# Strassen's algorithm for the second MLP product of a two-layer network, on one core

## Chip, core and metric

One core of a Trainium2 chip runs the whole program: 512 tokens of width 1024 through one block of attention, state-space mixing and an MLP, one RG-LRU layer and one latent-attention layer. The metric is the time of one execution on the device in microseconds (us), the median of several runs.

## What is computed

The change touches the MLP of the first block and the three norms around it:

```python
h2 = rms_norm(x, norm2_w[l]) * (1.0 + scale2) + shift2
ff = jnp.square(jax.nn.relu(h2 @ w_mlp1[l])) @ w_mlp2[l]
x = x + gate2 * ff
```

`h2` is 512 x 1024, `w_mlp1` 1024 x 4096, `w_mlp2` 4096 x 1024, and all is float32. After it the RG-LRU layer takes `rms_norm(x)` again, and the latent-attention layer once more.

## The kernel before

A float32 product is made of three passes of a faster format: each operand is split into a high part (a cast on ScalarE, `wh`, `rh`) and a low part (the operand minus the high part, `wl`, `rl`), and `mm3` (L173 to L176) adds hi x hi, hi x lo and lo x hi in PSUM. Each weight tile, 128x1024 (512 KB), is loaded by SP into `wr` (L159), cast on ScalarE (L162), and its low part is subtracted on VectorE or GpSimd (L165). `lo_pool` says how many of twelve go to GpSimd; in the MLP that is none. Four buffers each of `wr`, `wh` and `wl` let loads and splits run some blocks ahead of TensorE.

The MLP (`mlp`, L973) goes in 4 chunks of 1024 hidden units. The first product of a chunk (`gemm_cm`) has 8 blocks of 24 matmuls (8 k x 3) of 128 hidden units by 512 tokens. In chunk 0 the first four blocks are done by halves of the tokens, so that the norm of the last token blocks can still come in. Each block is followed by a relu on ScalarE (L982), a square on GpSimd (L983) and the split of the result (`split`, L167). The second product (`gemm_tm`) has two column halves x 4 token blocks x 8 k x 3 = 192 matmuls of 128 tokens by 512 columns. For each of its 8 sums, `resid` (L944) multiplies by the row of gates (L949) and adds to `x` (L950) on VectorE.

`token_norm` (L281) turns one block of 128 tokens of `x` into operands of the next product: two `xn` on GpSimd (L290), transposes on TensorE (L294), scaling and split. `half_stats` makes the sums that it needs (L322 to L328). `h2` is such an operand pair (two tiles, high and low), as are `ha` for RG-LRU and `hb` for latent attention; `norm2`, `norm3` and `norm4` make them.

No scheduler reorders: each engine runs its instructions in the order in which the program writes them, and waits for what they read and for their buffers. SP issues all loads in that order too. Pools (`phase`) decide what memory a tile reuses and so what it waits for.

Of the kernel before, what the change touches and what calls it, by code (L numbers as in the profile page):

```python
# [59 lines left out]
class Build:  # L60
# [1463 lines left out]
```

## Time and profile before

| what | value |
|---|---|
| median of 3 runs | 1649.78 us (1648.66 to 1652.85) |
| profiled execution | 1649.19 us, span 1647.4 us |
| mean granted clock of TensorE | 0.993 |
| busy: TensorE, VectorE, ScalarE, GpSimd | 96%, 68%, 48%, 27% |
| MLP, first matmul of product 1 to the end of chunk 3 | 867.5 to 1221.7 us |

A share is an average over the whole span. The MLP is some 354 us of it, and the views by stretch tell how busy each engine is there. In the rows below PE is TensorE's matmuls and PEld its weight loads, DVE is VectorE, ACT is ScalarE, POOL is GpSimd and SP issues loads; `out<-in` names the tiles, and an arrow behind a time names what ended the idle time before the instruction.

### The profile page before, as it was taken

Reading aid. Unit: us, or ns where it says so; the run is one execution under the profiler, and the core shown is the slowest. Engines: PE = TensorE matmul, PEld = TensorE weight load, DVE = VectorE, ACT = ScalarE, POOL = GpSimd, SP = SyncE. Lnnn points to the kernel's source line nnn. Section 1 sums busy time; section 2 is a strip of 40 time slices with the busy share of each in tenths; the row PEclk is TensorE's granted clock in tenths of the full one; section 3 lists DMA queues with packets and bytes.
Section 4 is the critical chain, followed back from the end, with each engine's and each line's share of the span. In section 5 each row is a group of like instructions: output and inputs, shape, how many; then the busy total and the mean of one; then the engine's idle time right before and its main releaser. Section 6 shows DMA issues by size and latency. Waiting matters only on the chain.

```text
span 1647.4 us, 20884 instructions
## 1 busy us (share of the span) xinstructions
PE 1580.8 (96%) x7696; PEld 1279.2 (78%) x7696; DVE 1128.2 (68%) x1948; ACT 789.3 (48%) x1517; POOL 446.0 (27%) x322
## 2 busy tenths in 40 slices
PE   5989999999999999999999999999999999999998
PEld 3767667677688778778888888888888778988886
DVE  7899679689868988874445343443467884747883
ACT  4356546354465667663334232232336662454652
POOL 3314335244252443431133011111141011321012
PEclk8999999999999999999999999999999999999999
DMA  7612124224222222315313333323323222322211
GB/s 254 196 52 65 52 77 128 75 72 139 91 82 80 80 62 80 96 52 183 111 52 117 101 97 95 102 90 102 105 77 99 87 90 67 100 69 69 65 63 52
DMA packets 50649, 153.54 MB, mean 93 GB/s; under 512 B 8178, under 2 KB 12914, under 8 KB 50547
## 3 DMA queue, kind: packets, MB, share of 16 engines
q1 hardware_dynamic: 50546, 152.22, 28.9%
q8 instruction: 60, 0.98, 0.3%
q14 instruction: 43, 0.34, 0.1%
HBM read 150.10 MB, written 2.10 MB: 92 GB/s over the span
## 4 chain that ended last, share of the span: by engine, by line
PE 67%; DVE 18%; ACT 4%; issue 3%; POOL 3%; DMA 1%; DVEq 0%; POOLq 0%; ACTq 0%
PE pm L175 18%; PE pm L174 18%; PE pm L176 18%; DVE acc L507 3%; DVE wl L165 1%; DVE nmax L752 1%; PE px L608 1%; PE px L848 1%; DVE w L635 1%; PE px L598 1%; DMA wada<-in_w_ada 1%; POOL rs L254 1%; PE px L857 1%; POOL wl L165 1%; PE px L856 1%
## 5 line engine op out<-in xcount | busy, mean ns | idle before, releaser
L162 ACT CAST wh<-wr 128x1024 fp32r<-128x1024 f32 (+5 forms) x245 | 239.7, 980 | 389.3 <-PE pm L175 168.9
L165 DVE TENSOR_TENSOR wl<-wr,wh 128x1024 fp32r<-128x1024 f32 (+2 forms) x170 | 203.3, 1196 | 184.8 <-ACT wh L162 183.9
L165 POOL TENSOR_TENSOR wl<-wr,wh 128x1024 fp32r<-128x1024 f32 (+3 forms) x75 | 174.7, 2330 | 532.9 <-ACT wh L162 486.6
L174 PE MATMUL pm<-hh,wh 128*128 128x512 f32 x432 | 173.8, 406 | 8.2 <-ACT hh L169 6.6
L175 PE MATMUL pm<-hl,wh 128*128 128x512 f32 x432 | 176.0, 407 | 3.9 <-POOL hl L170 3.8
L176 PE MATMUL pm<-hh,wl 128*128 128x512 f32 x432 | 172.9, 401 | 0.0
L983 POOL TENSOR_TENSOR r<-r 128x512 f32<-128x512 f32 x32 | 50.8, 1589 | 252.3 <-ACT r L982 252.3
L174 PE MATMUL pm<-h,wh 128*128 128x512 f32 (+1 forms) x288 | 105.4, 366 | 0.0
L175 PE MATMUL pm<-h,wh 128*128 128x512 f32 (+1 forms) x288 | 105.3, 365 | 0.0
L176 PE MATMUL pm<-h,wl 128*128 128x512 f32 (+1 forms) x288 | 105.2, 365 | 0.0
L174 PEld LDWEIGHTS pm<-hh,wh 128*128 128x128 f32 x432 | 81.8, 190 | 29.9 <-ACT hh L169 8.4
L175 PEld LDWEIGHTS pm<-hl,wh 128*128 128x128 f32 x432 | 82.3, 190 | 27.1 <-POOL hl L170 7.6
L174 PE MATMUL pm<-wh,rh 128*128 128x512 f32 x256 | 99.8, 390 | 0.0
L760 POOL TENSOR_SCALAR pr<-pr,psum 128x512 f32<-128x512 f32 x64 | 64.8, 1024 | 128.8 <-DVE psum L756 71.6
L176 PE MATMUL pm<-wh,rl 128*128 128x512 f32 x256 | 99.6, 389 | 0.0
L175 PE MATMUL pm<-wl,rh 128*128 128x512 f32 x256 | 99.6, 389 | 0.0
L176 PEld LDWEIGHTS pm<-hh,wl 128*128 128x128 f32 x432 | 82.4, 191 | 19.9 <-issue 3.1
L507 DVE SCALAR_TENSOR_TENSOR acc<-pm,conv_w_s,acc 128x510 f32<-128x510 f32 (+2 forms) x118 | 87.4, 741 | 8.3 <-ACT acc L498 7.3
L279 DVE SCALAR_TENSOR_TENSOR wada<-wada,cs 128x1024 f32<-128x1024 f32 x48 | 68.9, 1446 | 16.4 <-DMA wada<-in_w_ada 15.8
L643 POOL TENSOR_TENSOR e<-e,w 128x512 f32<-128x512 f32 x32 | 52.0, 1626 | 101.1 <-ACT e L642 87.0
L755 ACT ACTIVATE pr<-px,nmax 128x512 f32<-128x512 f32 (+2 forms) x96 | 60.5, 638 | 29.8 <-DVE nmax L752 23.9
L174 PE MATMUL pm<-ha,wh 128*128 128x512 f32 (+1 forms) x192 | 68.2, 355 | 0.0
(401 smaller groups left out, 4120.3 us busy)
## 6 DMA issues: line engine op xcount, KB each, us to landing
wr<-in_w_mlp SPq DMA_DIRECT2D x64, 512.0 KB, 3.5
wada<-in_w_ada SPq DMA_DIRECT2D x48, 512.0 KB, 4.0
wr<-in_w_xbc SPq DMA_DIRECT2D x24, 512.0 KB, 3.5
wr<-in_w_in_a SPq DMA_DIRECT2D x20, 512.0 KB, 3.5
wr<-in_w_z SPq DMA_DIRECT2D x16, 512.0 KB, 3.6
wr<-in_w_ssd_out SPq DMA_DIRECT2D x16, 512.0 KB, 3.6
wr<-in_w_gate SPq DMA_DIRECT2D x16, 512.0 KB, 3.7
wr<-in_w_qkv SPq DMA_DIRECT2D x16, 384.0 KB, 3.0
```

The lines of the kernel that those rows point to most:

```text
L162: nc.scalar.copy(out=hi[:, :n], in_=raw[:, :n])
L165: eng.tensor_tensor(out=lo[:, :n], in0=raw[:, :n], in1=r32(hi[:, :n]), op=ALU.subtract)
L174: m(out, lhsT=lh, rhs=rh, start=start, stop=False)
L175: m(out, lhsT=lh, rhs=rl, start=False, stop=False)
L176: m(out, lhsT=ll, rhs=rh, start=False, stop=stop)
L254: g.tensor_tensor(out=r, in0=r, in1=self.mhalf.to_broadcast(list(ss.shape)) if len(ss.shape) == 2 else self.mhalf.unsqueeze(2).to_broadcas ...
L279: nc.vector.scalar_tensor_tensor(out=w, in0=w, scalar=1.0, in1=self.cs, op0=ALU.mult, op1=ALU.mult, accum_out=self.modc[:, j:j + 1])
L507: nc.vector.scalar_tensor_tensor(out=acc[:, lo:hi], in0=ps[:, lo + o:hi + o], scalar=w[:, j:j + 1], in1=acc[:, lo:hi], op0=ALU.mult, op1=A ...
L643: self.e("ew").tensor_tensor(out=e, in0=e, in1=w, op=ALU.mult)
L755: nc.scalar.activation(out=e[:, :n], in_=p, func=AF.Exp, bias=nmax, accum_out=s)
L760: self.e("norm").tensor_scalar(out=e[:, :n], in0=e[:, :n], scalar1=s, scalar2=1.0, op0=ALU.mult, op1=ALU.mult)
L983: self.e("sq").tensor_tensor(out=r, in0=r, in1=r, op=ALU.mult)
```

## The change

The second product of each chunk becomes seven half-size products (Strassen's algorithm in Winograd's form) instead of eight. The squared hidden values `R` (1024 hidden units by 512 tokens) are cut into four quarters a11 to a22 by hidden half and token half, the weights `W0` and `W1` (the two column halves) into b11 to b22. A product is 2 token blocks x 4 k x 3 = 24 matmuls. Its two factors are made in place by additions of quarters (`combine`), and then split (`rparts`: 128x1024; `wparts`: two halves of 128x1024 each). Three of the products are added into PSUM tiles that already hold another (A and X), the rest into tiles of their own; each finished tile is added to `x` in one or two places.

The gate can no longer be multiplied into the sums, since one sum enters two column halves. It is multiplied into the raw weights on GpSimd (L1012 of the changed kernel), 8 tiles a chunk. The weights of the second product are loaded straight into `W0` and `W1`, one copy of each, so the loads of the next chunk go into quarters that the present one still reads. The low parts of R are made on VectorE for products 1 to 3 and on GpSimd for 4 to 7, all low parts of the weights on VectorE. Of the combinations, GpSimd has `a11-=a21` and the last of b11, VectorE the others.

The tiles `h2`, `ha` and `hb` share one pool of two (`hbig`). The rows of gates lie in another pool, some pools are entered at another point, pads between pools differ, and the small loads of the next layers come earlier. In the last chunk the sums are closed by token block, with the statistics and the next norm after each; the norms of token blocks 2 and 3 run inside the first product of RG-LRU. In the changed kernel the lines stand 3 lower up to the MLP (L165 becomes L168, L170 becomes L173).

```diff
-PAD = [0, 16, 56, 0, 32, 0, 32, 0, 0, 24, 0, 0, 40, 56, 32, 16, 0]
+PAD = [48, 16, 56, 0, 32, 0, 32, 32, 0, 0, 0, 0, 56, 0, 16, 0, 0]
...
+    def hbig(self, name):
+        return self.hpool.tile([128, 8, 512], F32R, tag="big", name=self.nm(name))
...
-        self.h2 = self.big("h2", F32R), self.big("h2", F32R)
+        self.h2 = self.hbig("h2"), self.hbig("h2")
...
-    def mlp(self, done):
+    def mlp(self):
...
         hh, hl = self.h2
+        R, W0, W1 = self.big("R"), self.big("W0"), self.big("W1")
+        a11, a21, a12, a22 = R[:, 0:4, 0:256], R[:, 0:4, 256:512], R[:, 4:8, 0:256], R[:, 4:8, 256:512]
+        b11, b21, b12, b22 = W0[:, 0:4], W0[:, 4:8], W1[:, 0:4], W1[:, 4:8]
+        V, P = nc.vector, nc.gpsimd
+        def rparts(x, eng):
+            hi, lo = [self.pool("x").tile([128, 4, 256], F32R, tag="x", name=self.nm(n)) for n in ("sh", "sl")]
+            self.split(hi, lo, x, eng=eng)
+            return hi, lo
+        def wparts(x, eng):
+            res = []
+            for j in (0, 2):
+                hi, lo = [self.pool(n).tile([128, 2, 512], F32R, tag=n, name=self.nm(n)) for n in ("wh", "wl")]
+                self.split(hi, lo, x[:, j:j + 2], eng=eng)
+                res += [(hi[:, k], lo[:, k]) for k in range(2)]
+            return res
+        def combine(out, x, y, op, eng, n=2):
+            for j in range(0, 4, n):
+                s = slice(j, j + n)
+                eng.tensor_tensor(out=out[:, s], in0=x[:, s], in1=y[:, s], op=op)
         for ch in range(4):
-            rt = []
+            for b, w in enumerate((W0, W1)):
+                for i in range(4):
+                    v = w[:, 2 * i:2 * i + 2]
+                    nc.sync.dma_start(out=v, in_=a["w_mlp2"][ch, b, i])
+                    gate = self.gb[40][:, b * 512:b * 512 + 512].unsqueeze(1).to_broadcast([128, 2, 512])
+                    P.tensor_tensor(out=v, in0=v, in1=gate, op=ALU.mult)
 
             def evac(m, ps):
-                with self.fills():
-                    r = self.t("r")
-                    hi, lo = self.t("rh", F32R), self.t("rl", F32R)
-                nc.scalar.activation(out=r, in_=ps, func=AF.Relu)
-                self.e("sq").tensor_tensor(out=r, in0=r, in1=r, op=ALU.mult)
-                self.split(hi, lo, r)
-                rt.append((hi, lo))
+                nc.scalar.activation(out=R[:, m], in_=ps, func=AF.Relu)
+                self.e("sq").tensor_tensor(out=R[:, m], in0=R[:, m], in1=R[:, m], op=ALU.mult)
 
             self.gemm_cm([[a["w_mlp1"][ch * 8 + m]] for m in range(8)], lambda k: (hh[:, k], hl[:, k]), evac,
-                         halves=4 if ch == 0 else 0, mid=lambda: self.norm2(3))
-            if ch == 3:
-                done()
...
-            self.gemm_tm([[a["w_mlp2"][ch, b, i] for i in range(4)] for b in range(2)], lambda k: rt[k],
-                         lambda b, t, ps: self.resid(self.gb[40], b, t, ps, self.r3 if ch == 3 else None), 512,
-                         touter=ch == 3, pre=self.trail(self.norm3) if ch == 3 else None)
+            Z, A, C, X = [[f(), f()] for f in (self.pm, self.pm, self.ps, self.ps)]
+            def product(r, w, ps, start, done):
+                (rh, rl) = r
+                order = [(j, i) for j in range(2) for i in range(2)] if not last or start else \
+                    [(j, i) for i in range(2) for j in range(2)]
+                for j, i in order:
+                    for k in (2 * j, 2 * j + 1):
+                        s = slice(i * 128, i * 128 + 128)
+                        self.mm3(ps[i], rh[:, k, s], rl[:, k, s], w[k][0], w[k][1], start and k == 0, k == 3,
+                                 skip_group_check=True)
+                    if j == 1:
+                        for tok, col in done:
+                            x = xv[:, tok * 2 + i, col * 512:col * 512 + 512]
+                            V.tensor_tensor(out=x, in0=x, in1=ps[i], op=ALU.add)
+                        if last:
+                            stats(ps, i)
+            def stats(ps, i):
+                t, n = (i, 0) if ps is C else (i, 1) if ps is X and X[0] in closing else \
+                    (i + 2, 2) if ps is A and A[0] in closing else (0, 3)
+                for b in [[0], [1], [0, 1], []][n]:
+                    self.half_stats(self.r3, xv[:, t, b * 512:b * 512 + 512], b, t)
+                if n == 2:
+                    self.norm3(i)
+            closing = []
+            combine(b12, b12, b11, ALU.subtract, V)
+            r, w = rparts(a11, V), wparts(b11, V)
+            product(r, w, A, True, [(0, 0)])
+            r, w = rparts(a12, V), wparts(b21, V)
+            product(r, w, C, True, [(0, 0)])
+            combine(a11, a11, a21, ALU.subtract, P, 4)
+            combine(a21, a21, a22, ALU.add, V, 4)
+            r, w = rparts(a21, V), wparts(b12, V)
+            product(r, w, X, True, [(1, 1)])
+            combine(b12, b22, b12, ALU.subtract, V)
+            combine(b21, b21, b12, ALU.subtract, V)
+            r, w = rparts(a22, P), wparts(b21, V)
+            product(r, w, Z, True, [(1, 0)])
+            combine(b11, b12, b11, ALU.subtract, P)
+            combine(a22, a22, a11, ALU.subtract, V, 4)
+            r, w = rparts(a22, P), wparts(b12, V)
+            product(r, w, A, False, [(0, 1)])
+            combine(a12, a12, a22, ALU.subtract, V, 4)
+            r, w = rparts(a12, P), wparts(b22, V)
+            closing = [X[0]]
+            product(r, w, X, False, [(0, 1)])
+            r, w = rparts(a11, P), wparts(b11, V)
+            closing = [A[0]]
+            product(r, w, A, False, [(1, 0), (1, 1)])
         self.dump("x2", xv)
...
-        self.hb = self.big("hb", F32R), self.big("hb", F32R)
+        self.hb = self.hbig("hb"), self.hbig("hb")
...
-                G = stack(b.phase(side="right"), tail)
-                b.gb = {j: b.c([128, 1024], f"gb{j}") for j in (16, 40)}
                 b.mh, b.ml = big("mh"), big("ml")
                 with b.fills():
                     b.merge()
                 O.close()
                 F.close()
+                H = stack(b.phase(nbig=2, side="right", bare=True), tail)
+                b.hpool = b.pool("big")
+                M = stack(b.phase(nt=NMLP, side="right"), tail)
+                b.gb = {j: b.c([128, 1024], f"gb{j}") for j in (16, 40)}
                 b.mod_cols(16, 32)
                 b.gate_rows(16, 0.5)
                 b.gate_rows(40, 1.0)
-                M = stack(b.phase(nt=NMLP, side="right"), tail)
-                H = stack(b.phase(nbig=2, side="right", bare=True), tail)
                 b.out_proj()
+            c = b.stack[0]["c"]
+            b.nkv, b.nb = b.load("norm_kv", [128, 8], pool=c), b.load("norm_b", [128, 8], pool=c)
+            b.lo_pool = LO["mlp"]
+            with b.phase(nbig=3, nx=6, bare=True):
+                b.mlp()
```

VectorE in the second product of a chunk, before: the low parts of the next first product's weights (L165), then the gates and sums.

```order
L165 TENSOR_TENSOR wl1746_8575<-wr1744_8573,wh1745_8574 128x1024
L165 TENSOR_TENSOR wl1753_8613<-wr1751_8611,wh1752_8612 128x1024
L165 TENSOR_TENSOR wl1760_8651<-wr1758_8649,wh1759_8650 128x1024
L949 TENSOR_TENSOR rt1739_8542<-pm1723_8436,gb40_6859 128x512
L949 TENSOR_TENSOR rt1740_8551<-pm1724_8437,gb40_6859 128x512
L950 TENSOR_TENSOR x1482_6847<-x1482_6847,rt1739_8542 128x512
L950 TENSOR_TENSOR x1482_6847<-x1482_6847,rt1740_8551 128x512
L949 TENSOR_TENSOR rt1741_8560<-pm1725_8438,gb40_6859 128x512
```

The same place now: product 3's weights (`wl1704`, `wl1706`), two in-place combinations of b12 (L1004 on W1) with sums of product 2 between them (L1039), b21 from b12 (on W0), a22 from a11 (on R), sums of product 3, and the first weight half of product 4 (`wl1710`).

```order
L173 TENSOR_TENSOR wl1704_8368<-W11642_7872,wh1703_8367 128x1024
L173 TENSOR_TENSOR wl1706_8372<-W11642_7872,wh1705_8371 128x1024
L1004 TENSOR_TENSOR W11642_7872<-W11642_7872 128x1024
L1039 TENSOR_TENSOR x1482_6849<-x1482_6849,px1685_8279 128x512
L1004 TENSOR_TENSOR W11642_7872<-W11642_7872 128x1024
L1039 TENSOR_TENSOR x1482_6849<-x1482_6849,px1686_8280 128x512
L1004 TENSOR_TENSOR W01641_7871<-W01641_7871,W11642_7872 128x1024 x2
L1004 TENSOR_TENSOR R1640_7870<-R1640_7870 128x4x256
L1039 TENSOR_TENSOR x1482_6849<-x1482_6849,px1687_8281 128x512
L1039 TENSOR_TENSOR x1482_6849<-x1482_6849,px1688_8282 128x512
L173 TENSOR_TENSOR wl1710_8410<-W01641_7871,wh1709_8409 128x1024
```

Six additions on SBUF operands now stand between the weights of product 3 and those of product 4.

GpSimd from the last norm ahead of the MLP, before: after the `xn` only squares follow, 32 in a row.

```order
L290 TENSOR_SCALAR xn1657_7974<-x1482_6847,r22_7476 128x512
L290 TENSOR_SCALAR xn1660_7988<-x1482_6847,r22_7476 128x512
L983 TENSOR_TENSOR r1663_8120<-r1663_8120 128x512
L983 TENSOR_TENSOR r1666_8127<-r1666_8127 128x512
L983 TENSOR_TENSOR r1669_8134<-r1669_8134 128x512
```

Now, from the squares of chunk 0 to those of chunk 1: `sl` are the low parts of R for products 4 to 7 (1708, 1714, 1720, 1726), L1004 is b11 from b12, L1012 the gates for the next chunk, first b21, then b12, b22 and b11.

```order
L1016 TENSOR_TENSOR R1640_7870<-R1640_7870 128x512 x4
L173 TENSOR_TENSOR sl1708_8406<-R1640_7870,sh1707_8405 128x1024
L1004 TENSOR_TENSOR W01641_7871<-W11642_7872,W01641_7871 128x1024 x2
L173 TENSOR_TENSOR sl1714_8447<-R1640_7870,sh1713_8446 128x1024
L1012 TENSOR_TENSOR W01641_7871<-W01641_7871,gb40_7443 128x1024 x2
L173 TENSOR_TENSOR sl1720_8486<-R1640_7870,sh1719_8485 128x1024
L1012 TENSOR_TENSOR W11642_7872<-W11642_7872,gb40_7443 128x1024
L173 TENSOR_TENSOR sl1726_8524<-R1640_7870,sh1725_8523 128x1024
L1012 TENSOR_TENSOR W11642_7872<-W11642_7872,gb40_7443 128x1024 x3
L1012 TENSOR_TENSOR W01641_7871<-W01641_7871,gb40_7443 128x1024 x2
L1016 TENSOR_TENSOR R1640_7870<-R1640_7870 128x512 x4
```

Two gates now stand ahead of product 6's low part, one ahead of product 7's, and five between that and the next chunk's squares.

VectorE at the start of the MLP, before: weights of the first product and the last parts of `h2` (the token blocks 2 and 3).

```order
L170 TENSOR_TENSOR h21573_7480<-nh1636_7840,h21572_7479 128x4x128
L165 TENSOR_TENSOR wl1653_7892<-wr1651_7890,wh1652_7891 128x1024
L170 TENSOR_TENSOR h21573_7480<-nh1639_7854,h21572_7479 128x4x128
L165 TENSOR_TENSOR wl1656_7898<-wr1654_7896,wh1655_7897 128x1024
L306 TENSOR_TENSOR nh1662_7995<-pt1661_7990,g2_7477 128x512
L309 TENSOR_TENSOR nh1662_7995<-nh1662_7995,modc_84 128x512
L170 TENSOR_TENSOR h21573_7480<-nh1659_7981,h21572_7479 128x4x128
L170 TENSOR_TENSOR h21573_7480<-nh1662_7995,h21572_7479 128x4x128
```

Now two combinations of W1 and W0 stand there; both read what GpSimd has multiplied by the gate.

```order
L173 TENSOR_TENSOR h21572_7475<-nh1638_7849,h21571_7474 128x4x128
L168 TENSOR_TENSOR wl1658_7913<-wr1656_7911,wh1657_7912 128x1024
L309 TENSOR_TENSOR nh1664_8010<-pt1663_8005,g2_7472 128x512
L1004 TENSOR_TENSOR W11642_7872<-W11642_7872,W01641_7871 128x1024
L173 TENSOR_TENSOR h21572_7475<-nh1661_7996,h21571_7474 128x4x128
L312 TENSOR_TENSOR nh1664_8010<-nh1664_8010,modc_85 128x512
L1004 TENSOR_TENSOR W11642_7872<-W11642_7872,W01641_7871 128x1024
L173 TENSOR_TENSOR h21572_7475<-nh1664_8010,h21571_7474 128x4x128
```

The low parts of `h2` for the last token block (from `nh1661` and `nh1664`) come behind them.

## Rows read from the trace of the kernel before

**Rows 1.** The page's first part: busy time, share of the span and instructions of each engine.

```profile
PE 1580.8 (96%) x7696; PEld 1279.2 (78%) x7696; DVE 1128.2 (68%) x1948; ACT 789.3 (48%) x1517; POOL 446.0 (27%) x322
```

**Rows 2.** Stretches of the MLP: stretch, length, busy us (instructions) per engine, clock, DMA share, GB/s.

```profile
913.30:956.80 43.50, 43.50 (x193) 36.04 (x192) 18.21 (x22) 9.52 (x10) 1.59 (x1) 1.00 0.30 97
956.80:1000.30 43.50, 43.50 (x193) 36.03 (x192) 16.55 (x19) 16.22 (x22) 11.13 (x7) 1.00 0.31 97
1130.90:1174.40 43.50, 43.50 (x193) 36.04 (x192) 16.52 (x19) 16.23 (x23) 11.12 (x7) 1.00 0.31 98
1174.40:1221.70 47.30, 46.35 (x218) 38.38 (x216) 27.96 (x54) 18.26 (x32) 13.17 (x18) 1.00 0.26 80
```

**Rows 3.** Waits in the MLP, 867 to 1222 us: total us, times, longest us.

```profile
POOL r L983 <- ACT r L982: 252.3, 32, 47.4
DVE wl L165 <- ACT wh L162: 132.7, 53, 4.2
ACT wh L162 <- PE pm L176: 102.1, 26, 4.4
...
PE pt L294 <- POOL xn L290: 2.3, 2, 1.3
```

**Rows 4.** Groups by line and shape, 867 to 1222 us: count, busy us, mean ns, idle before.

```profile
L174 PE MATMUL pm<-wh,rh 128*128 128x512 f32 x256 | 99.8, 390 | 0.0
...
L165 DVE TENSOR_TENSOR wl<-wr,wh 128x1024 fp32r<-128x1024 f32 x64 | 78.8, 1231 | 132.9 <-ACT wh L162 132.7 <-PE pm L175 0.3
L162 ACT CAST wh<-wr 128x1024 fp32r<-128x1024 f32 x64 | 67.3, 1054 | 158.8 <-PE pm L176 102.1 <-PE pm L175 52.6 <-issue 2.3
...
L983 POOL TENSOR_TENSOR r<-r 128x512 f32<-128x512 f32 x32 | 50.8, 1589 | 252.3 <-ACT r L982 252.3
...
L950 DVE TENSOR_TENSOR x<-x,rt 128x512 f32<-128x512 f32 x33 | 23.1, 734 | 0.0
...
L949 DVE TENSOR_TENSOR rt<-pm,gb 128x512 f32<-128x512 f32 x33 | 22.0, 685 | 9.7 <-PE pm L176 8.8
...
L982 ACT ACTIVATE r<-pm 128x512 f32<-128x512 f32 x32 | 18.9, 591 | 0.0
...
L290 POOL TENSOR_SCALAR xn<-x,r 128x512 f32<-128x512 f32 x9 | 10.5, 1173 | 0.4
```

**Rows 5.** Order of time, VectorE and GpSimd, 1440.6 to 1445.5: start us, us, instruction.

```profile
1440.69 1.21 DVE L165 TENSOR_TENSOR wl<-wr,wh 128x1024 fp32r<-128x1024 f32 x1
1441.83 1.21 DVE L161 TENSOR_TENSOR wr<-wr,norm_b_s 128x1024 f32<-128x1024 f32 x1
...
1440.88 4.41 POOL L165 TENSOR_TENSOR wl<-wr,wh 128x1024 fp32r<-128x1024 f32 x1 [4.72 <-ACT wh L162]
```

**Rows 6.** Order of time, GpSimd and VectorE, 837 to 842.

```profile
837.59 2.39 POOL L165 TENSOR_TENSOR wl<-wr,wh 128x1024 fp32r<-128x1024 f32 x1 [19.14 <-ACT wh L162]
837.77 0.69 DVE L949 TENSOR_TENSOR rt<-pm,gb 128x512 f32<-128x512 f32 x1 [4.45 <-PE pm L176]
...
838.50 2.03 DVE L950 TENSOR_TENSOR x<-x,rt 128x512 f32<-128x512 f32 x1
...
840.45 0.68 DVE L949 TENSOR_TENSOR rt<-pm,gb 128x512 f32<-128x512 f32 x1
```

**Rows 7.** The page's DMA issues: count, KB each, median us from issue to landing.

```profile
wr<-in_w_mlp SPq DMA_DIRECT2D x64, 512.0 KB, 3.5
```

**Rows 8.** Order of time, VectorE and GpSimd, 883.5 to 887.

```profile
884.03 1.23 DVE L165 TENSOR_TENSOR wl<-wr,wh 128x1024 fp32r<-128x1024 f32 x1 [3.66 <-ACT wh L162]
...
884.58 1.58 POOL L983 TENSOR_TENSOR r<-r 128x512 f32<-128x512 f32 x1 [10.16 <-ACT r L982]
```

**Rows 9.** Order of time, GpSimd from 861.3 and TensorE from 864, around the MLP's start.

```profile
861.38 0.58 POOL L327 TENSOR_SCALAR r<-r,r 128x1 f32<-128x1 f32 x1 [2.94 <-ACT sqj L322]
...
864.99 0.39 PE L176 MATMUL pm<-wh,ml 128*128 128x512 f32 x1
...
867.53 0.36 PE L174 MATMUL pm<-h,wh 128*128 128x256 f32 x1
867.74 0.28 PE L175 MATMUL pm<-h,wh 128*128 128x256 f32 x1
867.85 0.28 PE L176 MATMUL pm<-h,wl 128*128 128x256 f32 x1
```

**Rows 10.** Stretches of the first 42 us, columns as in Rows 2.

```profile
18.00:20.00 2.00, 0.26 (x3) 0.02 (x1) 1.18 (x5) 2.00 (x5) 0.00 (x0) 1.00 0.91 328
20.00:22.00 2.00, 0.74 (x2) 0.30 (x2) 1.56 (x2) 0.92 (x2) 1.00 (x1) 1.00 0.92 354
...
30.00:32.00 2.00, 2.00 (x5) 1.37 (x5) 1.90 (x5) 0.49 (x1) 0.29 (x1) 0.50 0.80 272
34.00:36.00 2.00, 2.00 (x10) 1.32 (x9) 2.00 (x3) 0.62 (x1) 1.05 (x2) 1.00 0.72 203
40.00:42.00 2.00, 1.35 (x6) 0.83 (x5) 2.00 (x3) 0.00 (x0) 1.23 (x1) 1.00 0.92 350
```

More of the change, by code (lines that the diff above doesn't have):

```diff
@@ L170, in split, with mm3 @@
         (eng or self.nc.vector).tensor_tensor(out=lo, in0=src, in1=r32(hi), op=ALU.subtract)
-    def mm3(self, out, lh, ll, rh, rl, start, stop):
+    def mm3(self, out, lh, ll, rh, rl, start, stop, **kw):
         m = self.nc.tensor.matmul
-        m(out, lhsT=lh, rhs=rh, start=start, stop=False)
-        m(out, lhsT=lh, rhs=rl, start=False, stop=False)
-        m(out, lhsT=ll, rhs=rh, start=False, stop=stop)
+        m(out, lhsT=lh, rhs=rh, start=start, stop=False, **kw)
+        m(out, lhsT=lh, rhs=rl, start=False, stop=False, **kw)
+        m(out, lhsT=ll, rhs=rh, start=False, stop=stop, **kw)
     def gemm_cm(self, blocks, rhs, evac, halves=0, kouter=0, gain=None, mid=None):
@@ L202, in gemm_cm @@
                                      k == 0, k == kt - 1)
-                        if mid and m == 0 and c0 == 0 and i == n - 2:
-                            mid()
+                        if mid and m == 0 and c0 == 0 and i < n - 1:
+                            mid(i)
             for i in range(n):
@@ L987, in mlp @@
             self.gemm_cm([[a["w_mlp1"][ch * 8 + m]] for m in range(8)], lambda k: (hh[:, k], hl[:, k]), evac,
-                         halves=4 if ch == 0 else 0, mid=lambda: self.norm2(3))
-            if ch == 3:
-                done()
+                         halves=4 if ch == 0 else 0, mid=lambda i: self.norm2(3) if i == 2 else None)
+            last = ch == 3
+            if last:
                 na = self.load("norm_a", [128, 8])
-                self.ha = self.big("ha", F32R), self.big("ha", F32R)
+                self.ha = self.hbig("ha"), self.hbig("ha")
@@ L993, in mlp @@
                 self.norm3 = self.token_norm(self.r3, *self.ha, na, key="xa")
-            self.gemm_tm([[a["w_mlp2"][ch, b, i] for i in range(4)] for b in range(2)], lambda k: rt[k],
-                         lambda b, t, ps: self.resid(self.gb[40], b, t, ps, self.r3 if ch == 3 else None), 512,
-                         touter=ch == 3, pre=self.trail(self.norm3) if ch == 3 else None)
+            Z, A, C, X = [[f(), f()] for f in (self.pm, self.pm, self.ps, self.ps)]
[12 more added lines that the diff above has]
+                            V.tensor_tensor(out=x, in0=x, in1=ps[i], op=ALU.add)
+                        if last:
+                            stats(ps, i)
@@ L1006, in rglru, with consts @@
         K = {}
-        def consts():
-            self.norm3(3)
+        def consts(i):
+            if i:
+                self.norm3(i + 1)
+            if i < 2:
+                return
             ready()
@@ L1402, in emit @@
                 b.rglru(ready)
-            tail.enter_context(b.phase(nq=8, side="right"))
+            inner.enter_context(b.phase(nq=8))
             with b.phase(nt=NMI):
@@ L1406, in emit @@
                 b.mla_in()
-            B.close()
+            H.close()
             with b.phase(nt=NMLA):
```

8 lines of the change are left out of this document (removed).

## Prediction

> **What bounds the kernel now.** I read the busy shares first: TensorE is busy for 96% of the span [rows 1], so the time is mostly its matmuls. Then the stretches of the MLP [rows 2]: in a second product TensorE is busy for 43.50 of 43.50 us, at full clock, and in a first product likewise. 192 matmuls in 43.5 us is 0.2266 us each (the 0.39 us shown for one overlaps the next). VectorE is busy for 16.5 to 18.3 of 43.5 us there and GpSimd for 1.6 to 11.1. Last the waits [rows 3]: the other engines wait for each other and for TensorE, TensorE itself for 2.3 us in all. So fewer matmuls shorten this stage, as long as the operands come in time.
>
> **What goes.** Each chunk's second product falls from 192 to 7 × 24 = 168 matmuls. 4 × 24 × 0.2266 = **21.8 us** off a path without gaps, the most that can be won. A half-size product takes 24 × 0.2266 = 5.44 us, seven 38.1 us.
>
> **What comes.** Per chunk, counted from the order of the changed kernel:
> - VectorE: 34 subtractions or additions of 128x1024 with both inputs in SBUF: 8 low parts of first weights, 14 of second weights, 3 of R, 6 half-combinations of W, 3 combinations of R. One takes 1.21 to 1.23 us, 1.14 from start to start [rows 4, 5]: 38.8 us. Also 16 adds from PSUM at some 0.60 (0.69 shown, pipelined) [rows 4]: 9.6 us.
> - GpSimd: 15 of 128x1024 (8 gate multiplies, 4 low parts, 3 combinations) at 2.39 us [rows 6]: 35.9 us, and 8 squares.
> - ScalarE: 21 casts of 1.05 us [rows 4] for the second product, beside 8 of the first and 8 relus of 0.59: some 35 us of 82, never the last to come. I cost it at nothing; its cover is the previous product, and without that a product would start one cast (1.05 us) later.
> - Loads: as many bytes as before, 512 KB each, 3.5 us to landing [rows 7]. They go straight into W0 and W1, so a load must wait until the last reader of that quarter is done.
>
> By busy time this fits. But [rows 6] show that these kinds of work don't lie beside each other. VectorE's `x<-x,rt`, 0.73 us on average [rows 4], took 2.03 us: it was held until GpSimd's subtraction ended at 839.98 and ended 0.55 us later. In [rows 5] it is the reverse: GpSimd's subtraction took 4.41 us, and its end, 1445.29, is 2.25 us after VectorE's second operation ended (1443.04). In [rows 8] a square started under a VectorE subtraction ended 0.90 us after it. So for operations with two SBUF inputs I let the two engines exclude each other wholly. An operation that takes PSUM isn't held: 837.77 took 0.69 us under a GpSimd subtraction [rows 6].
>
> Then the shared time of one chunk is 38.8 + 15 × 2.25 + 8 × 0.9 = **79.8 us**, against 43.5 + 38.1 = **81.6 us** of matmuls. Two full queues, each with dependences, cannot mesh to 98%.
>
> The Trainium skill (SBUF — State Buffer, "Who interferes with whom") states the same lock, but that whoever issues first gets the pair for the whole instruction; in [rows 5] GpSimd's was queued first and VectorE's next (1441.83) went ahead of it. By the page's order GpSimd would be held for one VectorE operation at most and my upper end would be some 7 us lower; the sum would stay.
>
> **The walk through a seven-product stage** (0 is the end of the first product). The last square is done at some 3.2: relu 0.59, square 1.59 [rows 4] and one hold of 1.14. From it VectorE runs, in the written order, 11 large operations and 6 adds to the first weight half of product 4: 11 × 1.14 + 6 × 0.6 = 16.1. GpSimd puts its low part of a22 and the two halves of the new b11 into the same stretch: 3 × 2.25 = 6.8, two of VectorE's adds, which take PSUM, run under them (-1.2). 3.2 + 16.1 + 6.8 - 1.2 = 24.9. Product 4 would be due at 3 × 5.44 = 16.3, so it is some **8.6 us** late.
> The next chunk's loads of b21 wait for the two low parts of product 4, land at about 28.4, and their two gate multiplies stand on GpSimd ahead of product 6's low part `sl1720`: 28.4 + 3 × 2.25 and VectorE's operations in between, 4 × 1.14, make 39.7, and one matmul's lead-in 40. Product 6 was due at 24.9 + 2 × 5.44 = 35.8 and is **4.2 us** late. Product 7 loses one more hold, **2.2 us**, to the third gate ahead of `sl1726`. A stage takes 38.1 + 15.0 = 53.1 us, where it was 43.5. In the last chunk no gates follow: 38.1 + 8.6 + 0.6 (product 7 behind the statistics of the closing sums, one small operation) = 47.3.
> After a stage with gates, the weights' low part for block 1 of the next first product stands behind a combination that waits for the last gates (five of them come after `sl1726`, 11 us and more): **3 us**, three times.
>
> **The start.** The first W load waits for the last w_o matmul, which ends at 865.4 [rows 9], and lands at 868.9. GpSimd then does gate 1, two small operations and two `xn` for token block 3 (0.58 and 1.17 each [rows 4, 9]), gates 2 to 6: 6 × 2.4 + 3.5 = 17.9, so 886.8, with VectorE in between 888. VectorE's two half-combinations, which wait for gates 5 and 6, stand ahead of the low parts of h2 that the second column halves of blocks 0 to 3 need: some 890. The first halves end 4 × 24 × 0.12 = 11.5 us after 867.5 [rows 9], at 879. **11 us** of TensorE idle.
>
> **Other edits.** The end of the MLP now has its last sums closed by product 7, and the transposes of blocks 2 and 3 ahead of the first RG-LRU matmul: bounds 0 (as now, 2 us of gaps) and 6 (one chain of two small operations, two `xn`, a cast and two subtractions on [rows 4, 9]: 1.2 + 2.3 + 0.6 + 1.4, and 0.5 of transposes). I take 0. Earlier loads of small constants, the shared pool and the pads: 0, since SP's loads in [rows 7] land in 3.5 us and blocks wait 5.44 us for each; bounds 0 to 1 us.
> The clock: in the first 40 us the granted clock fell to 0.50, its lower level of 1.2 GHz, after TensorE had been busy for 0.26 and 0.74 of two stretches of 2 us, and was at 1.00 again at 34 [rows 10]. At 0.50 a matmul took 0.40 us (5 in 2 us). If ten or so matmuls after each long idle ran so, at 0.40 for 0.227, that is 2 us each, for five idles of 8 to 11 us: 0 to 10 us. I take 0, the other row with idle in it (40 to 42) having kept 1.00, and leave the 10 for the range.
>
> **Sum:** 3 × 15.0 + 9.2 + 3 × 3 + 11 − 21.8 = +52.4 on the profiled execution's 1649.19 us (span 1647.4 and 1.8 around it; 0.6 below the median): **1702 us**, slower.
> Its own range: down to 1674, if GpSimd's three operations fall into VectorE's adds and waits (−3.7 a stage) and the gates never delay product 6 (−4.2 three times); up to 1726, with the clock (10), the end (6) and GpSimd losing a second VectorE operation at each gate ahead of product 6 (7).
>
> **Rivals.**
> 1. No lock that matters: VectorE and GpSimd go side by side. For it: their busy shares are low. Against: [rows 5, 6, 8]. VectorE's chain of 16.1 us alone still makes product 4 late by 3 (4 × 3 = 12), and the start costs 9.5, being GpSimd's own time. 1649.2 − 21.8 + 21.5 = 1649, no change. Chance 0.07.
> 2. The other side: everything is ready in time, the full gain, 1627 us. It is decided at product 4: where its first weight half's low part is done 16.3 us into the stage. For it: in [rows 2] VectorE idles for more than half, and splits run several blocks ahead. Against: the four combinations before it can't begin before product 3's low parts are read. With a part of the stalls, still faster: 1627 to 1644. Chance 0.11.
> 3. The lock costs what I say and the clock falls in the gaps too: 1712 to 1728. Chance 0.12.
> That the change doesn't do less work is excluded: the order has 7 × 24 matmuls a chunk.
>
> **How the numbers follow.** A measurement of this kernel can tell about 0.3%, 5 us. Forecast 0.70, with rival 3 0.82 slower; rival 1, 0.07 the same; rival 2, 0.11 faster. The range 1648 to 1728 takes in the forecast with its bounds, rival 3 and half of rival 1; outside lie rival 2, the rest of rival 1 and what is above.
>
> **What would show it.** Right: the stretch from the first matmul of product 1 to the last of 7 at 50 to 55 us in chunks 0 to 2, 46 to 49 in chunk 3; TensorE idle some 8 us before product 4, waiting for VectorE's low part; the mean of the weight low parts well above 1.23 and of the gates above 2.39; 11 us idle near 879. Wrong: stages of 39 to 41 us, or gates and subtractions overlapping at their own durations.

## The result and the profile after

The changed kernel takes **1733.55 us** (median of 4 runs, 1731.59 to 1735.10) for 1650.49 before: a ratio of 1.050 (95% interval 1.048 to 1.052), 83 us slower. The profiled execution took 1734.1 us, span 1732.2, at a mean granted clock of 0.968 for 0.993. Forecast: 1702, range 1648 to 1728. The sign was right, the size was not, and the time lies above the range.

The first part of the page after answers to [rows 1]: VectorE is busy for 151 us longer and GpSimd for 167 us. TensorE is busy for 12.9 us longer although 96 matmuls are gone.

```profile
PE 1593.7 (92%) x7600; PEld 1279.4 (74%) x7600; DVE 1279.0 (74%) x1989; ACT 820.2 (47%) x1537; POOL 612.7 (35%) x381
```

The stretches of the MLP answer to [rows 2], columns as there. A stage is a chunk's seven half-size products. In order: the first product of chunk 0, the stage of chunk 0, the first product of chunk 1, the stage of chunk 3, and the gap to RG-LRU.

```profile
867.70:930.10 62.40, 49.39 (x298) 44.76 (x297) 30.10 (x21) 16.82 (x26) 38.20 (x20) 0.86 0.34 124
930.10:981.20 51.10, 41.69 (x169) 32.54 (x169) 48.79 (x33) 20.38 (x21) 32.30 (x12) 0.93 0.26 83
981.20:1032.10 50.90, 45.34 (x193) 37.08 (x192) 22.86 (x19) 12.91 (x16) 23.05 (x12) 0.93 0.26 83
1239.90:1293.60 53.70, 44.67 (x178) 35.04 (x177) 47.37 (x39) 25.65 (x35) 27.68 (x21) 0.87 0.08 25
1293.60:1301.30 7.70, 2.37 (x18) 1.79 (x16) 7.26 (x10) 4.04 (x9) 6.66 (x8) 0.92 0.32 87
```

In the stage (930 to 981) VectorE is busy for 48.8 of 51.1 us, the time in which GpSimd holds it included, where it was 18 of 43.5: it has become the bound. The three first products after a stage take 50.8 to 52.1 us instead of 43.5, that of chunk 0 62.4 instead of 45.5. What TensorE waited for, 867 to 1302 us (it was 2.3 us in all, [rows 3]):

```profile
PE pm L177 <- ACT wh L172: 19.4, 4, 4.8
PE pm L179 <- DVE wl L168: 16.3, 3, 5.6
PE pm L178 <- DVE h L173: 11.8, 1, 11.8
...
PE px L179 <- POOL sl L173: 5.2, 3, 1.7
```

Groups of the MLP by line and shape (answering to [rows 4]): a low part of W takes 2.04 us instead of 1.23, a gate on GpSimd 2.86, where its subtraction of the same size took 2.39 in [rows 6]; the sums, which read PSUM, take 0.68, as such an operation did before (L949).

```profile
L173 DVE TENSOR_TENSOR wl<-W,wh 128x1024 fp32r<-128x1024 f32 x56 | 112.7, 2043 | 48.9 <-ACT wh L172 48.9
L1012 POOL TENSOR_TENSOR W<-W,gb 128x1024 f32<-128x1024 f32 x32 | 90.7, 2860 | 9.5 <-DMA W<-in_w_mlp 9.2
...
L1039 DVE TENSOR_TENSOR x<-x,pm 128x512 f32<-128x512 f32 x40 | 25.8, 676 | 2.5 <-PE pm L179 2.5
```

Where product 4 waits, in order of time: VectorE, then GpSimd, then ScalarE and TensorE.

```profile
942.22 1.21 DVE L1004 TENSOR_TENSOR W<-W 128x1024 f32<-128x1024 f32 x1
943.36 0.67 DVE L1039 TENSOR_TENSOR x<-x,px 128x512 f32<-128x512 f32 x1
943.95 3.03 DVE L1004 TENSOR_TENSOR W<-W 128x1024 f32<-128x1024 f32 x1
946.91 0.67 DVE L1039 TENSOR_TENSOR x<-x,px 128x512 f32<-128x512 f32 x1
947.51 4.12 DVE L1004 TENSOR_TENSOR W<-W,W 128x1024 f32<-128x1024 f32 x2
951.55 1.21 DVE L1004 TENSOR_TENSOR R<-R 128x1024 f32<-128x1024 f32 x1
```

```profile
943.51 2.40 POOL L1004 TENSOR_TENSOR W<-W,W 128x1024 f32<-128x1024 f32 x1 [3.43 <-DVE W L1004]
947.07 2.35 POOL L1004 TENSOR_TENSOR W<-W,W 128x1024 f32<-128x1024 f32 x1 [1.16 <-DVE W L1004]
```

```profile
950.60 3.13 ACT L172 CAST wh<-W 128x1024 fp32r<-128x1024 f32 x3 [12.15 <-DVE W L1004]
946.48 0.39 PE L179 MATMUL px<-wh,sl 128*128 128x512 f32 x1
951.70 1.04 PE L177 MATMUL pm<-wh,sh 128*128 128x512 f32 x2 [4.84 <-ACT wh L172]
954.73 1.22 PE L177 MATMUL pm<-wh,sh 128*128 128x512 f32 x2 [1.99 <-ACT sh L172]
```

GpSimd's subtraction from 943.51 to 945.91 and VectorE's of 943.95 (3.03 us) meet: VectorE's ends 1.07 us, about its own length, after GpSimd's. Those of 947.07 and 947.51 (two on VectorE) meet in the same way. Product 3 ends at 946.9; TensorE gets the high part of product 4's weights at 951.70, since its cast (950.60) waits for the combination of 947.51, and it waits again for the next cast until 954.73: 8.0 us late.

### The profile page after: what moved, and what is told of

It reads as the page before. It is cut to its first block, busy times and chain, and to the rows that moved or that the text cites. A ratio compares the mean times of both kernels' runs of the same rounds, so it can differ in the third digit from the quotient of the medians.

```text
span 1732.2 us, 20842 instructions
## 1 busy us (share of the span) xinstructions
PE 1593.7 (92%) x7600; PEld 1279.4 (74%) x7600; DVE 1279.0 (74%) x1989; ACT 820.2 (47%) x1537; POOL 612.7 (35%) x381
## 4 chain that ended last, share of the span: by engine, by line
PE 52%; DVE 24%; POOL 8%; ACT 5%; issue 5%; DMA 2%; DVEq 0%; SPq 0%; POOLq 0%; ACTq 0%
PE pm L178 14%; PE pm L177 14%; PE pm L179 13%; POOL W L1012 4%; DVE acc L510 3%; DVE wl L168 2%; DVE W L1004 2%; DVE nmax L755 1%; DVE wl L173 1%; DVE w L638 1%; POOL sl L173 1%; PE px L611 1%; PE px L851 1%; PE px L601 1%; DVE th L519 1%
## 5 line engine op out<-in xcount | busy, mean ns | idle before, releaser
L165 ACT CAST wh<-wr 128x1024 fp32r<-128x1024 f32 (+5 forms) x213 | 206.1, 970 | 348.3 <-PE pm L178 208.1
L168 POOL TENSOR_TENSOR wl<-wr,wh 128x1024 fp32r<-128x1024 f32 (+4 forms) x74 | 173.8, 2350 | 550.8 <-ACT wh L165 502.3
L168 DVE TENSOR_TENSOR wl<-wr,wh 128x1024 fp32r<-128x1024 f32 (+5 forms) x139 | 173.3, 1250 | 85.3 <-ACT wh L165 83.9
L173 DVE TENSOR_TENSOR wl<-W,wh 128x1024 fp32r<-128x1024 f32 x56 | 112.7, 2043 | 48.9 <-ACT wh L172 48.9
L178 PE MATMUL pm<-h,wh 128*128 128x512 f32 (+1 forms) x288 | 108.6, 378 | 11.8 <-DVE h L173 11.8
L172 ACT CAST wh<-W 128x1024 fp32r<-128x1024 f32 x56 | 58.0, 1048 | 109.5 <-PE pm L178 51.2
L177 PE MATMUL pm<-h,wh 128*128 128x512 f32 (+1 forms) x288 | 109.0, 379 | 0.7 <-ACT h L172 0.7
L1012 POOL TENSOR_TENSOR W<-W,gb 128x1024 f32<-128x1024 f32 x32 | 90.7, 2860 | 9.5 <-DMA W<-in_w_mlp 9.2
L1016 POOL TENSOR_TENSOR R<-R 128x512 f32<-128x512 f32 x32 | 53.9, 1683 | 103.7 <-ACT R L1015 103.7
L646 POOL TENSOR_TENSOR e<-e,w 128x512 f32<-128x512 f32 x32 | 52.1, 1628 | 100.3 <-ACT e L645 86.3
L177 PE MATMUL pm<-wh,sh 128*128 128x512 f32 x128 | 56.0, 450 | 26.8 <-ACT wh L172 19.4
L179 PEld LDWEIGHTS pm<-h,wl 128*128 128x128 f32 x288 | 57.2, 199 | 26.8 <-DVE wl L168 17.6
```

What stands on the lines that cost most here:

```text
L165: nc.scalar.copy(out=hi[:, :n], in_=raw[:, :n])
L168: eng.tensor_tensor(out=lo[:, :n], in0=raw[:, :n], in1=r32(hi[:, :n]), op=ALU.subtract)
L172: self.nc.scalar.copy(out=hi, in_=src)
L173: (eng or self.nc.vector).tensor_tensor(out=lo, in0=src, in1=r32(hi), op=ALU.subtract)
L177: m(out, lhsT=lh, rhs=rh, start=start, stop=False, **kw)
L178: m(out, lhsT=lh, rhs=rl, start=False, stop=False, **kw)
```

## Experiments

The kernel before took 1647.7 to 1649.4 us beside these runs. A stage, from the first matmul of product 1 to the last of product 7, took 51.0, 52.2, 52.6 and 53.6 us in the change, with 43.5 before (45.3 in chunk 3) and 38.0 without a wait.

**No gates.** Without the line `P.tensor_tensor(out=v, in0=v, in1=gate, op=ALU.mult)`, so that the sums are added ungated.

> The changed kernel without the 32 multiplications of the second weights by the row of gates (the sums are added ungated); all else stays. Theory (GpSimd's gates hold VectorE by the shared port and its in-order queue): the 13 us idle at the start, the 5.6 us idle in block 1 of three first products and about 3 us a stage ahead of products 6 and 7 go, with the low clock behind each (4 us, then some 2 us each); the 8 us ahead of product 4 stay. 1733 - 17 - 23 - 10 = 1683 us, 1675 to 1692. Rival (the gates lie beside other work and the chain of additions on VectorE alone makes the stalls): at most 10 us less, 1723 or more.

1680.1 us (ratio 1.0185, 1.0168 to 1.0202), as the theory had it. The first products take 45.8 and three times 43.5, the stages 47.1 to 48.2 and 52.0. The 8 us ahead of product 4 are unchanged.

**The first combination behind the low parts.**

```diff
-            combine(b12, b12, b11, ALU.subtract, V)
+            combine(b12, b12, b11, ALU.subtract, V, pin=True)
```

> The first combination of each chunk (b12 less b11) is queued on VectorE behind the low parts of all eight blocks of the first product, where the program has it; nothing else moves. Theory (VectorE's queue stands still at this combination until GpSimd has done the gates): the 13 us idle at the start go with some 4 us of low clock, and 5.6 us idle and 2 us of low clock in block 1 of three first products: 1733 - 17 - 23 = 1693 us, 1685 to 1702. Rival (the low parts are held by the port while the gates run, whatever their order): more than half of the idle stays, 1713 or more.

1698.3 us (1.0281 to 1.0315), as the theory had it: 35 us of the loss are the place of one combination (two instructions a chunk) in VectorE's queue. The first products are 43.48 again, the first one 50.6, the stages stay at 52 to 54. In the trace of the change, at the start, one sees it stand (VectorE; 887.05 is the combination):

```profile
878.48 0.69 DVE L309 TENSOR_TENSOR nh<-pt,g 128x512 f32<-128x512 f32 x1 [2.90 <-PE pt L297]
887.05 3.35 DVE L1004 TENSOR_TENSOR W<-W,W 128x1024 f32<-128x1024 f32 x1 [7.88 <-POOL W L1012]
890.32 2.82 DVE L173 TENSOR_TENSOR h<-nh,h 128x512 fp32r<-128x512 f32 x1
893.07 2.85 DVE L312 TENSOR_TENSOR nh<-nh,modc 128x512 f32<-128x512 f32 x1
895.84 1.21 DVE L1004 TENSOR_TENSOR W<-W,W 128x1024 f32<-128x1024 f32 x1
```

From 879.2 to 887.05 VectorE does nothing; behind the combination stand the low parts of `h2`, and TensorE is idle from 881.4 to 893.2. Block 1 of the next first product, VectorE and then TensorE, with a stretch of 2 us behind its wait (the granted clock is the third number from the end):

```profile
987.66 3.34 DVE L1004 TENSOR_TENSOR W<-W,W 128x1024 f32<-128x1024 f32 x1 [5.80 <-POOL W L1012]
993.04 0.79 PE L179 MATMUL pm<-h,wl 128*128 128x512 f32 x1 [5.56 <-DVE wl L168]
994.00:996.00 2.00, 2.00 (x6) 1.55 (x5) 2.00 (x5) 0.00 (x0) 0.00 (x0) 0.50 0.76 254
```

**Matmuls that keep the clock up.**

```diff
+            for _ in range(32):
+                nc.tensor.matmul(Z[0], lhsT=hh[:, 0, 0:128], rhs=hh[:, 0], start=True, stop=True)
             product(r, w, Z, True, [(1, 0)])
```

> Ahead of product 4 TensorE runs 32 matmuls whose result is not used (7.3 us at 0.227), inside the 8 us in which it waits. Theory (the low clock in the stage is the cost of the long idle time): the clock stays at 1.00 in the stage, the 2.4 to 4.9 us a stage of slow matmuls go, 14 us in all; 1719 us, 1716 to 1727. Rival (the clock falls for another reason, or the matmuls only add): 1733 to 1745.

A miss: 1735.7 us (1.0503 to 1.0540). In the change the clock falls in the wait ahead of product 4 (stretches of 2 us):

```profile
950.00:952.00 2.00, 0.30 (x1) 0.30 (x2) 2.00 (x3) 1.31 (x2) 0.00 (x0) 0.98 0.00 0
952.00:954.00 2.00, 0.74 (x2) 0.00 (x1) 2.00 (x4) 2.00 (x3) 0.00 (x0) 0.50 0.00 0
956.00:958.00 2.00, 2.00 (x6) 1.52 (x6) 2.00 (x1) 0.00 (x0) 1.32 (x1) 0.50 0.82 246
960.00:962.00 2.00, 2.00 (x11) 1.63 (x10) 2.00 (x2) 0.71 (x1) 1.76 (x1) 1.00 0.88 264
```

With the added matmuls it is 1.00 from 944 to 968 us in chunk 0, through this wait and products 4 and 5. But then it falls in the waits at product 6:

```profile
970.00:972.00 2.00, 0.42 (x1) 0.42 (x2) 2.00 (x2) 2.00 (x3) 2.00 (x2) 0.50 0.00 0
972.00:974.00 2.00, 2.00 (x6) 1.52 (x6) 2.00 (x3) 0.74 (x1) 2.00 (x2) 0.50 0.72 213
```

The stages of chunks 0 to 2 take 54.6 us each, longer than in the change, and the first products behind them 47.1 to 50.0, shorter. TensorE's longest waits there (two stages and the first product between them):

```profile
PE px L178 <- DVE wl L173: 4.1, 2, 2.1
PE pm L179 <- DVE wl L168: 3.3, 1, 3.3
```

In the change the first of them was 0.8 us and the second 5.6. So full speed through products 4 and 5 won nothing, since TensorE reached product 6 no earlier (38.0 us into the stage for 36.8 to 37.7) and waited there. What the low clock costs in a stage this run does not tell: the clock fell again, and GpSimd's queue had one more gate ahead of product 7's low part than in the change.

**GpSimd's other work to VectorE.** `V, P = nc.vector, nc.gpsimd` becomes `V = P = nc.vector`; gates and squares stay on GpSimd.

> All of GpSimd's combinations and low parts of R go to VectorE (8 instructions a chunk more there); the gates and squares stay on GpSimd. Theory (the two engines exclude each other, so an operation costs VectorE 2.25 on GpSimd and 1.14 on itself): the wait ahead of product 4 falls from 8 to about 4 us, the gates end some 9 us earlier, so that products 6 and 7 and block 1 of the next first product wait less: 1733 - 16 - 10 - 9 - 8 (clock) = 1690 us, 1680 to 1712. Rival (no exclusion, VectorE's own queue is too long): 8 x 1.14 more in each stage, 1740 or more.

1709.7 us (1.0347 to 1.0384), within the range, by other ways than expected: the waits at product 4 fall from 6.8 us (4.8 and 2.0) to 2.6, and block 1 doesn't wait any more (43.48), but the stages stay at 52.8, 54.5, 52.7 (49.6 in chunk 3): product 5 now waits 5.0 us for its low part, and the gates run inside the stage and hold VectorE at products 5 and 6.

**Gates behind the stage.** As the second run, with `keep_in_program_order` on the gates: all eight then stand on GpSimd behind the last low part of the stage.

> As the run with the first combination behind the low parts, and the gates of the next chunk are queued on GpSimd behind all its other work of the seven-product stage, so that they run beside the next first product, which has slack. Theory (each gate inside the stage holds VectorE by the shared port): the stages of chunks 0 to 2 fall from 52.3 us to the 47.5 they took without gates, the first products stay at 43.5: 1698 - 3 x 4.8 = 1684 us, 1678 to 1692. Rival (VectorE's own chain sets the length of the stage): 52 us as before, 1695 to 1702.

1687.8 us (1.0220 to 1.0246), as the theory had it: stages of 48.2 to 48.5 (52.0 in chunk 3), first products at 43.48. The wait for GpSimd's low part at product 6, 2.1 us in the second run, is gone.

**What the engines share.** The run without gates, with four multiplications and four writes of a constant a chunk, in turn, on a tile that nobody reads:

```diff
+            for q in range(8):
+                g = self.gb[40].rearrange("p (a b) -> p a b", a=2)
+                self.tc.keep_in_program_order(P.memset(scr, 0.0) if q % 2 else P.tensor_tensor(out=scr, in0=g, in1=g, op=ALU.mult))
```

> The run without gates (the second weights are not multiplied by the row of gates), with 8 more operations of 128x1024 on GpSimd a chunk, on a tile that nobody reads, beside the first product: four multiply two SBUF operands, four only write a constant, in turn. Theory (what the engines share is the way that reads SBUF operands): VectorE's low parts that meet a multiplication take up to 3.4 us, those that meet a constant 1.22. Rival (any work of GpSimd slows VectorE): both kinds take longer than 1.22.

One execution, 1695.3 us, taken for its trace. GpSimd, then VectorE, where each kind is met:

```profile
1240.47 0.95 POOL L1076 MEMSET scr<- 128x1024 f32 x1
1241.51 2.30 POOL L1076 TENSOR_TENSOR scr<-gb 128x1024 f32<-128x1024 f32 x1
1243.87 0.95 POOL L1076 MEMSET scr<- 128x1024 f32 x1
```

```profile
1240.83 1.23 DVE L168 TENSOR_TENSOR wl<-wr,wh 128x1024 fp32r<-128x1024 f32 x1 [1.73 <-ACT wh L165]
...
1242.57 2.32 DVE L168 TENSOR_TENSOR wl<-wr,wh 128x1024 fp32r<-128x1024 f32 x1
```

The low part of 1240.83 has its 1.23 us under a memset. That of 1242.57 meets the multiplication, ends 1.08 us after its end at 1243.81, and doesn't mind that the next memset runs in that time. In the trace this is the one place with a subtraction that meets a memset alone; at all others it meets a multiplication first and ends some 1.1 us after that, with a memset beside it.

**All on VectorE, the combinations ahead of the stage.** Two tiles more (t2, t4); gates after blocks 0 to 3 of the first product, combinations after blocks 4 to 6:

```diff
+                for b, j in {0: [(1, 0), (1, 2)], 1: [(0, 0), (0, 2)], 2: [(1, 4), (1, 6)], 3: [(0, 4), (0, 6)]}.get(m, []):
...
+                    pin(V.tensor_tensor(out=v, in0=v, in1=gate, op=ALU.mult))
+                for out, x, y in {4: [(b12, b12, b11)], 5: [(t2, b22, b12)], 6: [(t4, b21, t2)]}.get(m, []):
```

> GpSimd keeps only the squares: gates, combinations and all low parts are VectorE's, the gates and the three combinations of W that lead to products 3 to 5 are queued between the blocks of the first product, and b22-(b12-b11) and b21 less that have tiles of their own. Count on VectorE: some 28 operations x 1.14 and 12 to 16 sums x 0.60 inside a stage = 40, about 31 us of 43.5 beside the first product. Theory (port and queue were the whole loss): stages of 38.5 to 41 us, no idle beside the first products and at the start, the end as in the change (8 us): 1649 - 4 x 4 + 8 = 1641 us, 1632 to 1652. Rival (the low clock or PSUM sums make the stage long in any case): stages of 45 and more, 1660 or more.

**1640.1 us**, ratio 0.9952 (0.9936 to 0.9968), as the theory had it: 93 us less than the change, and 0.5% less than the kernel before, a small gain, but with an interval clear of 1. Stage and first product of chunk 0 and 1, stage of chunk 3, gap to RG-LRU:

```profile
915.80:953.80 38.00, 38.00 (x169) 31.49 (x168) 35.70 (x39) 20.96 (x21) 1.59 (x1) 1.00 0.39 125
953.90:997.40 43.50, 43.50 (x194) 36.02 (x193) 34.66 (x28) 12.94 (x16) 12.57 (x7) 1.00 0.30 97
1160.60:1200.60 40.00, 39.37 (x177) 32.24 (x176) 35.99 (x39) 25.10 (x34) 8.68 (x13) 1.00 0.11 30
1200.60:1208.00 7.40, 2.72 (x18) 2.11 (x18) 6.92 (x9) 4.62 (x11) 7.13 (x7) 0.87 0.34 101
```

TensorE is busy for 38.00 of 38.00 us in the stage and VectorE for 35.7. What is left is the end: 40.0 in the last stage and 7.4 in the gap, where it was 2.2.

**Squares to ScalarE** (`AF.Square` in place of GpSimd's product).

> As the run before, and the squares are ScalarE's (8 x 0.6 a chunk), so GpSimd does nothing between two norms. Theory (each square holds VectorE for some 0.9 to 1.3 us, but only the last one of a chunk is in the way): 0 to 2 us a chunk less, 0 to 8 in all. Rival (ScalarE, with some 40 us of casts in 82, becomes late): 2 us or more slower.

1637.9 us, 0.9934 (0.9921 to 0.9946). The difference to the run before is inside both intervals; the first product of chunk 0 is 45.5 for 46.9.

**VectorE's chain without GpSimd.** As two runs before (squares on GpSimd), but the combinations in place and in the stage.

> As the run with all on VectorE (squares on GpSimd), but the combinations of W that lead to products 3 to 5 stay in place inside the seven-product stage, the first behind the low parts of the first product: VectorE's chain of the change, without GpSimd beside it. It parts the two halves of the 9 to 14 us by which a stage of the change is longer than 38.1. If the shared port makes most of it: the wait ahead of product 4 is 3 us, stages of 41 to 43, 1640 + 4 x 4 = 1656 us, 1650 to 1662. If VectorE's chain makes most of it: stages of 46 and more, 1670 or more.

1679.2 us (1.0163 to 1.0197), the second of the two outcomes. Stages of 48.3 to 48.4, and 49.6 in chunk 3, though every operation of VectorE takes its own 1.22 us. Product 4 waits 2.6 us (3 expected); product 5 waits another 2.6, which I had not counted. TensorE at product 4 and 5, then VectorE:

```profile
1025.94 0.72 PE L178 MATMUL pm<-wl,sh 128*128 128x512 f32 x1 [2.61 <-DVE wl L173]
1035.87 0.50 PE L178 MATMUL pm<-wl,sh 128*128 128x512 f32 x1 [2.60 <-DVE wl L173]
```

```profile
1029.21 1.22 DVE L1004 TENSOR_TENSOR R<-R 128x1024 f32<-128x1024 f32 x1
1031.49 0.69 DVE L1044 TENSOR_TENSOR x<-x,pm 128x512 f32<-128x512 f32 x1 [1.06 <-PE pm L179]
1032.86 0.69 DVE L1044 TENSOR_TENSOR x<-x,pm 128x512 f32<-128x512 f32 x1 [0.67 <-PE pm L179]
1033.46 1.22 DVE L173 TENSOR_TENSOR sl<-R,sh 128x1024 fp32r<-128x1024 f32 x1
1034.59 2.35 DVE L173 TENSOR_TENSOR wl<-W,wh 128x1024 fp32r<-128x1024 f32 x2
```

After 1030.43 VectorE waits for TensorE: the sums of product 4 (1031.49, 1032.86) stand ahead of product 5's low parts, so these begin when product 4 is nearly over. And product 4 is slow: from 1026 to 1030, behind its wait, the granted clock is 0.51 and 0.63. This run's order differs from the change's there (in the change two of the low parts stand ahead of the sums), and all that GpSimd did in the stage is now VectorE's, so it does not part port and chain to the last us.

**The end.** As the run with the squares on ScalarE, with the transposes of token blocks 2 and 3 pinned behind RG-LRU's first blocks, without and with GpSimd's low part among the norms.

> As the run with all on VectorE and the squares on ScalarE, and at the end of the MLP: the transposes of token blocks 2 and 3 are queued on TensorE behind the first two blocks of the RG-LRU product (halves of the tokens), and GpSimd gets no low part of its first four weights. Theory (the 8 us lost at the end are transposes that stand ahead of matmuls whose operands are there, held by a low part on GpSimd among the norms): the gap between the last chunk and RG-LRU falls from 7.3 to 2 us, the slow clock behind it goes: 1638 - 7 = 1631 us, 1628 to 1635. Rival (RG-LRU waits for the low parts of its own operand or weights): 1635 to 1640.

> Of the run before only the order on TensorE; GpSimd keeps its low part among the norms. Theory: most of the gain is the order, since the transposes that wait for the held xn then stand behind matmuls that can run: 1633 us, 1629 to 1636. If the held xn alone was the cause: 1635 to 1639, with the gap moved to the transposes of block 2.

1638.5 (0.9921 to 0.9952) and 1637.8 us (0.9922 to 0.9951): no gain that shows. The gap falls from 7.4 to 4.6 and 4.2 us, but RG-LRU's first product, 26.6 us, then takes 27.4 and 27.8. The rival holds: TensorE now waits 3.3 and 2.9 us for the high part of RG-LRU's own operand (`ha`, cast on ScalarE). What would shorten the end stays open.

## Why the prediction was right and wrong

Against the times of [rows 2], on the profiled executions:

| term | forecast | measured |
|---|---|---|
| stages of chunks 0 to 2, over 38.1 | 15.0 each | 12.9, 14.1, 14.5 |
| stage of chunk 3, over 38.1 | 9.2 | 15.5 |
| first products after a stage | 3 each | 7.4, 8.6, 7.3 |
| start | 11 | 16.9 |
| end | 0 | 8.0 (gap 5.5, RG-LRU 2.5) |

The measured rows and the 21.8 us make 83.4 of the 84.9 us. Of the last stage's 15.5 us 1.8 were there before (it took 45.3 us then, not 43.5, which the forecast's sum overlooked too). Some 2.6 us are lost in the latent-attention layer, in the traces of the changed kernel and of runs made from it alike; their cause stays open: a stretch of 100 matmuls that took 16.5 us takes 18.4 to 18.5.

**Right:** the 21.8 us are there to be won (in the runs without a wait each of three stages is 38.04); VectorE and GpSimd exclude each other, and product 4 comes 8.0 us late (8.6 forecast), by way of the casts behind VectorE's combination; the combination that waits for gates holds the start and block 1, in the places named, and at the start for 11.8 us (11 forecast).

**The steps that failed** are sizes, 31 us together (with the first three stages, which came out 3.5 us shorter, taken off). (1) "**3 us**, three times": block 1 waits 5.2 to 5.6 us, since the combination waits 5.8 us for a gate and then for the end of the next one (987.66, 3.34 us for 1.22), and TensorE then runs its first matmuls at the low clock: 7.3 to 8.6 us each. (2) "The clock ... I take 0": what the waits at the start and at block 1 leave unexplained, 2 to 4 us each, goes with stretches like 994 to 996 above, 6 matmuls in 2 us at a granted 0.50, the lower level of 1.2 GHz. The start costs 16.9 us for 11, though its wait was right. In the second run start and block 1 gave back 35 us, for which the forecast had 11 + 9 = 20. (3) The last stage, where I had 0.6 us for product 7 behind the statistics: without gates it still takes 52.0 us, 3.8 more than the stage before it. In the change the transposes inside product 7 wait 0.7 and 1.1 us for GpSimd, and from 1290 to 1292 the clock is 0.50 behind them. (4) "I take 0" for the end: 8 us, beyond the bound of 6 that I gave. The upper end of the forecast's own range, 1726, was added up wrongly by a little, too: 1702 with 10, 6 and 7 is 1725.

**Right by the sum, in part by luck:** of the 15.0 us in a stage I had 8.6 at product 4 and 6.4 at products 6 and 7. In the trace some 10 us are lost by the start of product 5 (the 8.0 and slow matmuls behind them) and 3.4 to 4.4 after it: two misses that cancel. I charged the lock with most and VectorE's chain with 3. At product 4 that is borne out: with GpSimd's combinations and low parts on VectorE (fourth run, run of VectorE's chain) it waits 2.6 us for 6.8. But the chain's run gains little by it: its stage still needs 10.3 us more than 38.0, as VectorE has that work to do itself and product 5 now waits for it. The gates inside the stage are worth some 4 us (52.3 to 48.3), by the lock or by standing ahead of GpSimd's low parts; no run parts the two. What the lock costs by itself is thus not shown, since no run has the same work on both engines without it. Shown is that the place of VectorE's work decides: 39 us between the chain's run and the one with the combinations ahead, in tiles of their own (that of b11 also moved, one place later). Rival 1 is out: the subtractions of 943.95 and 947.51 and the run with reads and writes show the lock.

The port: [rows 5, 6, 8] and the run with reads and writes agree with the Trainium skill (SBUF — State Buffer, "Who interferes with whom"): a GpSimd instruction that only writes doesn't hold VectorE (1.23 us beside a memset, 2.32 beside a multiplication). On the order of the two, the same section of the Trainium skill, "whoever issues first", fits the stage, where both engines take turns and an operation lasts about as long as one of each (2.35 and 1.1 us), better than it fits [rows 5]. GpSimd, then VectorE, in the change:

```profile
972.87 3.38 POOL L173 TENSOR_TENSOR sl<-R,sh 128x1024 fp32r<-128x1024 f32 x1
977.26 3.41 DVE L168 TENSOR_TENSOR wl<-wr,wh 128x1024 fp32r<-128x1024 f32 x1
```

One sentence of the section on the kernel before is wrong: that no scheduler reorders. A scheduler orders each engine's queue when the program is built. The text has the first combination behind the low parts of all eight blocks; in the trace of the change it stands at 887.05, ahead of the last four of them in chunk 0 (901.51 to 909.75), and at 987.66, ahead of seven in chunk 1. That is the combination that cost 35 us.

## What to carry to other kernels

A product that saves matmuls pays in operations on its operands: count them per stage on the engine that does them, and put what doesn't depend on the stage ahead of it, in tiles of its own; that was worth 39 us here, more than the saving. Work given to GpSimd was no relief for VectorE here, where both read SBUF: 1.22 us on the one is 2.4 on the other, and the one waits for the other (combinations and low parts of R back on VectorE: 1709.7 for 1733.6 us). And look for the instruction in a queue that waits for another engine: everything behind it waits too.

## What was not expected of the hardware

Keeping TensorE's clock at 1.00 through the wait ahead of product 4 gave nothing (1735.7 for 1733.6 us): TensorE reached product 6 no earlier, waited there 1.6 us for a cast and 2.1 us for a low part, and the clock fell to 0.50 in those waits (970 to 976 us).
